# First layer: shift and scale by halves of the features, x's tiles loaded between them, the first half applied meanwhile

## The chip, the cores and the metric

The kernel runs on one core of a Trainium2 chip. The metric is the device time of one execution in microseconds, lower is better. TensorE (PE), VectorE (DVE), ScalarE (ACT), GpSimd (POOL) and the DMA queue of SyncE (SP) each run a program of their own in order and wait for each other by semaphores.

## The reference, cut to what matters

Two layers (`DEPTH = 2`) over 256 context tokens and 1024 latent tokens of 1024 features, batch 1, all in float32. At the head of each layer stands a normalisation with a shift and a scale that are themselves products of a vector with a large weight (`w_mod[l]` is 1024 x 3072, 12.6 MB):

```python
mod = jax.nn.silu(c) @ w_mod[l] + b_mod[l]
mod_c = jax.nn.silu(c_ctx) @ w_mod[l] + b_mod[l]
sh, sc, gt = jnp.split(mod, 3, axis=-1)
sh_c, sc_c, gt_c = jnp.split(mod_c, 3, axis=-1)
hx = _rms(x, norm_w[l]) * (1.0 + sc[:, None, :]) + sh[:, None, :]
hc = _rms(ctx, norm_w[l]) * (1.0 + sc_c) + sh_c
ux = _split(hx @ w_in[l], [M_COLS, A_COLS, G_COLS, D_COLS])
uc = _split(hc @ w_in[l], [M_COLS, A_COLS, G_COLS, D_COLS])
...
x = x + gt[:, None, :] * (yx @ w_out[l])
```

Between the two products four mixers (mLSTM, differential attention, GLA, gated DeltaNet) work on the columns. The change touches only `sh`, `sc`, `hx` and `hc` of the first layer.

## The kernel before, in words

**Order of the program.** The kernel is written as strands (`Strand`, threads at build time). A planner (`Issue`) asks every strand for its next instruction, estimates when its inputs and its engine are ready, and lets the earliest go first, with a rank per strand to break ties (`RANK`). `q_.need(...)` makes a strand wait until another has called `q_.set(...)` of the same name; this orders the program only, the chip waits by the tiles that an instruction reads and writes. All instructions pass through one helper line (L406), so the profile is read by tile names. All loads and stores go through one queue (`dma`, SP), in program order, and a load whose buffer is still in use holds up what stands behind it there. On the chip each load also waits until the load eight places ahead of it has landed, since eight semaphores go round.

**Start of the first layer (`first_norm`).** The 1280 tokens are ten tiles of 128 (tiles 0 and 1 are context), in three groups `GRP` of 2, 4 and 4 tiles. Three strands work side by side:

- `modulations`: `modulation(l, part, c0, n, ...)` makes one part (0 is the shift, 1 the scale, 2 the gate) for `n` features from `c0`. It loads eight row blocks `wm` of `w_mod`, multiplies each with the 2 columns of `cvec` (both vectors, latent and context) into a bank `mod`, copies the two rows to SBUF (`wm`, DVE), turns them with small transposes (PE), and writes columns of `AB[0]` (`md`, then `AB`, DVE). For the first layer the parts 0 and 1 are made whole, 1024 features at a time, with five buffers `wm` of 512 KB.
- `norms`: `normed(t)` loads the tile `x` (three buffers), squares and sums it on ACT (`junk`, `ss`), takes the power -1/2 on POOL (`ss`) and scales `x` on DVE. From the fourth tile on the strand waits for "w_mod loads", that is until the last `wm` load is in the program.
- `turns`: `turn(t, x)` transposes the tile in two times four blocks (`tr<-k_ident,x`, PE) and copies them to `flat[g]` (`f<-tr`, DVE or ACT).

Then the body goes over group and block of 128 features (`todo`, 24 steps): apply scale and shift on DVE (`f<-f,AB`), round on ACT (`hT<-f`, the high part), subtract on POOL or DVE (`hT<-f,hT`, the low part). The order is all eight blocks of a group, then the next group, and the whole loop waits for `(0, "AB")`, both parts.

**What follows (`Proj`).** The projection `mm<-hT,w` multiplies a group's `hT` with the split weights `w`; for one unit of columns that is 24 products per group, group 0 first. A finished bank is copied out by ACT (`st<-mm`) and some of it is stored (`dkr<-st`). After `first_norm` is done, the remaining modulations (gate of the first layer, all of the second) run in 256 KB loads between the products.

Of the kernel before, what the change touches and what calls it, by code (L numbers as in the profile page):

```python
# [22 lines left out]
DM = 1024  # L23
# [12 lines left out]
GRP = ((0, 2), (2, 4), (6, 4))  # L36
# [393 lines left out]
def _build(tc, nc, A, out, root, dbg):  # L430
    q_ = Issue()
# [34 lines left out]
    def mark(label):  # L466
        if q_.me:
            q_.me.label = label

    def dma(dst, src):  # L470
        SP.dma_start(out=dst, in_=src)

    def evac(dst, src, scale=None):
        n = math.prod(src.shape[1:])
        if q_.now["S"] + 0.1 + n / 1200 <= q_.now["V"] + n / 960:
            if scale is None:
                S.copy(dst, src)
            else:
                S.activation(dst, src, AF.Copy, scale=scale)
        elif scale is None:  # L480
            V.tensor_copy(dst, src)
        else:
            V.tensor_scalar(dst, src, scale, None, ALU.mult)

    def sub(dst, a, b):
        n = math.prod(a.shape[1:])
        if q_.now["G"] + 2.2e-3 * n <= q_.now["V"] + n / 960:
            G.tensor_tensor(dst, a, b, ALU.subtract)
        else:
            V.tensor_tensor(dst, a, b, ALU.subtract)  # L490
# [30 lines left out]
    def rsqrt_small(dst, src, mul, eps):  # L521
        V.tensor_scalar(dst, src, mul, eps, ALU.mult, ALU.add)
        shp = list(dst.shape)
        mh = mhalf[:shp[0], 0:1]
        while len(mh.shape) < len(shp):
            mh = mh.unsqueeze(1)
        G.tensor_tensor(dst, dst, mh.to_broadcast(shp), ALU.pow)
# [49 lines left out]
    def pc(l, key, i=0, n=1):  # L577
        return pcol[:, l, PR[key] + i:PR[key] + i + n]
# [27 lines left out]
    AB = [cst([128, 2, 2, 8], f"AB{l}") for l in L2]  # L606

    def xin(l, t):
        if l:
            return x1[t]  # L610
        if t < NCT:
            return A["ctx"][0, 128 * t:128 * t + 128, :]
        return A["x"][0, 128 * (t - NCT):128 * (t - NCT) + 128, :]


    def modulation(l, part, c0, n, p, pps, bufs):

        ps = pps([128, 256], "mod")
        for k in range(8):
            w = p([128, n], "wm", bufs)  # L620
            dma(w, A["w_mod"][l, 128 * k:128 * k + 128, 1024 * part + c0:1024 * part + c0 + n])
            if (l, part, k) == (0, 1, 7):
                q_.set("w_mod loads")
            for j in range(n // 256):
                P.matmul(ps[32 * j:32 * j + 2], cvec[:, k, :], w[:, 256 * j:256 * j + 256],
                         start=(k == 0), stop=(k == 7), tile_position=(0, 32 * j))
        q_.need(("params", l))
        rows = p([128, n], "wm", bufs)[:2].rearrange("p (a b) -> p a b", b=256)
        for j in range(n // 256):
            V.tensor_copy(rows[:, j, :], ps[32 * j:32 * j + 2])  # L630
        if part < 2:
            m, k0 = n // 128, c0 // 128
            pt = pps([128, 256], "mod")
            for j in range(m):
                P.transpose(pt[:, 2 * j:2 * j + 2], rows[:, j // 2, 128 * (j % 2):128 * (j % 2) + 128], ident[:2, :2])
            md = p([128, 8, 2], "md")[:, :m]
            V.tensor_tensor(md, pt[:, :2 * m].rearrange("p (k v) -> p k v", v=2),
                            pc(l, "bm", 8 * part + k0, m).unsqueeze(2).to_broadcast([128, m, 2]), ALU.add)
            for v in range(2):
                if part == 1:  # L640
                    V.scalar_tensor_tensor(AB[l][:, 0, v, k0:k0 + m], md[:, :, v], 1.0, pc(l, "nw", k0, m), ALU.add, ALU.mult)
                else:
                    V.tensor_copy(AB[l][:, 1, v, k0:k0 + m], md[:, :, v])
        else:
            brow = p([128, n], "wm", bufs)[:2]
            dma(brow, A["b_mod"][l:l + 1, 2048 + c0:2048 + c0 + n].to_broadcast([2, n]))
            rv = rows.rearrange("p a b -> p (a b)")
            V.tensor_tensor(rv, rv, brow, ALU.add)
            dma(gtd[l][:, c0:c0 + n], rv)

    def first_norm(hT):

        mark("0norm")
        st3 = ExitStack()
        fp = Pool(st3, "flat", side="right")
        flat = [fp([128, 8, 128 * n], f"f{g}") for g, (t0, n) in enumerate(GRP)]

        def modulations():
            mark("0mod")
            with ExitStack() as st:  # L660
                mp, mps = Pool(st, "wm", side="right"), Pool(st, "mps", PSUM, "right")
                for part in range(2):
                    modulation(0, part, 0, DM, mp, mps, 5)
            q_.set((0, "AB"))
            q_.need((0, "normed"))

            q_.me.rank = RANK["mod"]
            with ExitStack() as st:
                mp, mps = Pool(st, "wm"), Pool(st, "mps", PSUM)
                q_.set((0, "room"))  # L670
                for l, part in ((0, 2), *((l, part) for l in layers if l for part in range(3))):
                    for c0 in (0, 512):
                        modulation(l, part, c0, 512, mp, mps, 3)
                if "d" in parts:
                    q_.need((0, "front"))
            q_.set("modulated")
        q_.spawn(0, modulations)
        if True:
            st2 = ExitStack()
            xp, pps = Pool(st2, "xn"), Pool(st2, "nps", PSUM)  # L680

            def normed(t):
                x = xp([128, DM], "x", 3)
                dma(x, xin(0, t))
                junk = xp([128, DM], "junk")
                ss = xp([128, 2], "ss", 4)
                S.activation(junk, x, AF.Square, accum_out=ss[:, 0:1])
                rsqrt_small(ss[:, 1:2], ss[:, 0:1], 1.0 / DM, EPS)
                V.tensor_scalar(x, x, ss[:, 1:2], None, ALU.mult)
                return x  # L690

            def turn(t, x):
                g = next(g for g, (t0, n) in enumerate(GRP) if t0 <= t < t0 + n)
                o = 128 * (t - GRP[g][0])
                for h in range(2):
                    ps = pps([128, 512], "tr", 2)
                    for i in range(4):
                        P.transpose(ps[:, 128 * i:128 * i + 128], x[:, 128 * (4 * h + i):128 * (4 * h + i) + 128], ident)
                    evac(flat[g][:, 4 * h:4 * h + 4, o:o + 128], ps.rearrange("p (a b) -> p a b", b=128))
            xs = {}  # L700

            def norms():
                mark("0norm")
                for t in range(NT):
                    if t > 2:
                        q_.need((0, "turned", t - 3), "w_mod loads")
                    xs[t] = normed(t)
                    q_.set((0, "normed", t))
            q_.spawn(1, norms)

            def turns():
                mark("0norm")
                for t in range(NT):
                    q_.need((0, "normed", t))
                    turn(t, xs[t])
                    q_.set((0, "turned", t))
            q_.spawn(1, turns)
        q_.need((0, "AB"))
        todo = [(g, k) for g in range(len(GRP)) for k in range(8)]
        for i in range(len(todo) + 2):  # L720
            if i < len(todo):
                g, k = todo[i]
                q_.need((0, "turned", GRP[g][0] + GRP[g][1] - 1))
                x, v = flat[g][:, k, :], 1 if g == 0 else 0
                V.tensor_scalar(x, x, AB[0][:, 0, v, k:k + 1], AB[0][:, 1, v, k:k + 1], ALU.mult, ALU.add)
            if 0 < i <= len(todo):
                g, k = todo[i - 1]
                S.copy(hT[0][g][:, k, :], flat[g][:, k, :])
            if i > 1:
                g, k = todo[i - 2]  # L730
                sub(hT[1][g][:, k, :], flat[g][:, k, :], hT[0][g][:, k, :])
                if k == 7:
                    q_.set((0, "h", g))
        st2.close()
        st3.close()
        q_.set((0, "normed"))
# [463 lines left out]
    def right():  # L1200

        for L in LY:
# [5 lines left out]
            if l == 0:  # L1208
                first_norm(L.hT)
                q_.need("consts")  # L1210
                pst.close()
# [1724 lines left out]
```

## Time and profile before

| | |
|---|---|
| median of 3 runs | 2420.31 us (2413.67 to 2424.84) |
| profiled execution | 2405.2 us, span of the core 2403.3 us |
| mean granted TensorE clock | 0.942 |
| PE busy | 2113.9 us, 88% of the span |
| DVE, ACT, POOL busy | 62%, 41%, 35% |
| DMA | 335.38 MB, mean 140 GB/s |

A group of the profile reads: line, engine, operation, out<-in, count, then busy time, mean time of one, and the idle time of the engine just ahead of it with what ended it. In a timeline row the first number is the start in us and the second the time; a bracket tells how long the engine had been idle and what released it. A matmul of float32 is recorded as two passes.

### The profile page before, as it was taken

The numbers are of one execution on the slowest core, as the hardware profiler recorded it, in microseconds if no ns is written. First come the engines' busy times: TensorE is split into PE (matmuls) and PEld (weight loads), VectorE is DVE, ScalarE is ACT, GpSimd is POOL, SyncE is SP. The second block draws the span as 40 slices with busy tenths as digits, with TensorE's granted clock in tenths as the row PEclk, the third lists the DMA queues.
The fourth block names the chain that finished last, engine by engine and source line by source line (L and its number), as shares of the span: only waits on it lengthen the run. The fifth ranks groups of instructions, "written<-read, shape, count | busy, mean of one in ns | idle before, by whom it ended". The sixth has DMA issues, their size and how long they took to land. (4 is left out here: it accounts for less than half of the span.)

```text
span 2403.3 us, 57716 instructions
## 1 busy us (share of the span) xinstructions
PE 2113.9 (88%) x23367; PEld 1737.7 (72%) x23367; DVE 1500.8 (62%) x2726; ACT 981.6 (41%) x2168; POOL 834.4 (35%) x1048
## 2 busy tenths in 40 slices
PE   5898999999898998888877888889999889976888
PEld 1656778888776677876765668888788667775776
DVE  3586669555386863537666476696633778655475
ACT  2346412433276763213334264313322667632240
POOL 1244523555122224332431244433433122255240
PEclk7899999999999999989989899999999999986999
DMA  7347643445513116258963236433444431164595
GB/s 264 108 140 233 192 147 102 146 146 161 161 44 93 53 51 166 67 128 252 280 214 114 70 108 189 135 113 100 144 124 125 120 98 35 50 170 99 155 302 184
DMA packets 348053, 335.38 MB, mean 140 GB/s; under 512 B 93147, under 2 KB 292283, under 8 KB 347275
## 3 DMA queue, kind: packets, MB, share of 16 engines
q1 hardware_dynamic: 347786, 331.69, 46.1%
q8 instruction: 185, 3.03, 0.5%
q14 instruction: 82, 0.66, 0.1%
HBM read 226.78 MB, written 107.43 MB: 139 GB/s over the span
## 5 line engine op out<-in xcount | busy, mean ns | idle before, releaser
L406 PE MATMUL mm<-w,hT 128*128 128x256 f32 x4512 | 641.2, 293 | 17.6 <-DVE st L406 10.2
L406 PEld LDWEIGHTS mm<-w,hT 128*128 128x128 f32 x4512 | 576.1, 193 | 50.4 <-issue 20.5
L406 PE MATMUL mm<-hT,w 128*128 128x512 f32 (+1 forms) x1680 | 388.8, 377 | 20.3 <-ACT w L406 5.9
L406 PEld LDWEIGHTS mm<-hT,w 128*128 128x128 f32 x1680 | 283.2, 194 | 91.9 <-issue 20.8
L406 DVE TENSOR_REDUCE st<-sc 128x1 f32<-128x1024 f32 (+1 forms) x200 | 200.0, 1026 | 66.8 <-PE sc L406 65.6
L406 ACT ACTIVATE p<-sc,st 128x256 f32<-128x256 f32 (+1 forms) x272 | 211.3, 786 | 68.3 <-DVE st L406 51.7
L406 POOL TENSOR_TENSOR w<-wr,w 128x512 fp32r<-128x512 f32 x54 | 80.7, 1495 | 275.3 <-ACT w L406 220.9
L406 POOL TENSOR_TENSOR hss<-hss,mhalf 128x2 f32<-128x2 f32 (+2 forms) x72 | 104.1, 1446 | 157.1 <-DVE hss L406 143.1
L406 PE MATMUL o<-wo,yT 128*128 128x512 f32 x540 | 148.9, 412 | 4.8 <-DVE x L406 3.2
L406 PE MATMUL sc<-KT,qt 96*128 96x512 f32 (+1 forms) x400 | 124.2, 400 | 29.8 <-DMA KT<-akh 12.9
L406 ACT COPY wt<-tr 128x512 f32<-128x512 f32 (+1 forms) x200 | 102.2, 511 | 66.0 <-PE tr L406 65.6
L406 ACT COPY st<-mm 128x512 f32<-128x512 f32 (+1 forms) x81 | 44.9, 554 | 204.2 <-PE mm L406 142.0
L406 POOL TENSOR_TENSOR ss<-ss,mhalf 128x1 f32<-128x1 f32 (+1 forms) x39 | 68.4, 1754 | 168.9 <-DVE ss L406 168.7
L406 PEld LDWEIGHTS o<-wo,yT 128*128 128x128 f32 x540 | 102.1, 195 | 29.6 <-DVE x L406 3.8
L406 PE MATMUL tr<-k_ident,p 128*128 128x128 f32 x656 | 115.2, 281 | 7.5 <-ACT wt L406 7.0
L406 POOL TENSOR_TENSOR st<-st 128x1 f32<-128x1 f32 (+1 forms) x136 | 27.1, 199 | 270.8 <-ACT p L406 190.4
L406 ACT CAST w<-wr 128x512 fp32r<-128x512 f32 x128 | 77.4, 622 | 98.0 <-PE mm L406 56.7
L406 PE MATMUL po<-wt,av 128*64 128x128 f32 x1312 | 105.3, 284 | 3.5 <-DVE aacc L406 3.5
L406 PEld LDWEIGHTS sc<-KT,qt 96*128 96x128 f32 x400 | 63.6, 196 | 58.9 <-ACT p L406 30.9
L406 DVE SCALAR_TENSOR_TENSOR p<-p,st,p 128x1280 f32<-128x1280 f32 (+1 forms) x72 | 103.0, 1430 | 2.5 <-POOL st L406 2.3
L406 PE MATMUL o<-w,yT 128*128 128x512 f32 x324 | 100.9, 439 | 4.0 <-DVE st L406 4.0
L406 DVE TENSOR_TENSOR w<-wr,w 128x512 fp32r<-128x512 f32 x74 | 68.1, 922 | 54.5 <-ACT w L406 54.3
(314 smaller groups left out, 4062.8 us busy)
## 6 DMA issues: line engine op xcount, KB each, us to landing
wr<-in_w_in SPq DMA_DIRECT2D x64, 512.0 KB
wm<-in_w_mod SPq DMA_DIRECT2D x64, 256.0 KB
y<-y SPq DMA_DIRECT2D x36, 256.0 KB
xp<-st SPq DMA_DIRECT2D x18, 512.0 KB
pd<-rs_NG SPq DMA_DIRECT2D x18, 512.0 KB
kq<-kq SPq DMA_DIRECT2D x18, 512.0 KB
x<-xp SPq DMA_DIRECT2D x18, 512.0 KB
wm<-in_w_mod SPq DMA_DIRECT2D x16, 512.0 KB
```

Of the source, the lines that this page charges most:

```text
L406: r = fn(*a, **k)
```

## The change

The parts 0 and 1 of the first layer are made in two halves of 512 features, shift and scale of the first half, then of the second, with ten buffers of 256 KB in place of five of 512 KB (the same space). The body no longer waits for both parts as a whole: it goes over the halves outermost, and a step needs only its own half (`(0, "AB", k // 4)`) and its group's tiles. The tiles of x no longer wait for the last `wm` load.

```diff
@@ modulation
             dma(w, A["w_mod"][l, 128 * k:128 * k + 128, 1024 * part + c0:1024 * part + c0 + n])
-            if (l, part, k) == (0, 1, 7):
-                q_.set("w_mod loads")
             for j in range(n // 256):
@@ modulations
-                for part in range(2):
-                    modulation(0, part, 0, DM, mp, mps, 5)
-            q_.set((0, "AB"))
+
+                for hf in range(2):
+                    for part in range(2):
+                        modulation(0, part, 512 * hf, 512, mp, mps, 10)
+                    q_.set((0, "AB", hf))
@@ norms
-                        q_.need((0, "turned", t - 3), "w_mod loads")
+                        q_.need((0, "turned", t - 3))
@@ body
-        q_.need((0, "AB"))
-        todo = [(g, k) for g in range(len(GRP)) for k in range(8)]
+        todo = [(g, k) for hf in range(2) for g in range(len(GRP)) for k in range(4 * hf, 4 * hf + 4)]
         for i in range(len(todo) + 2):
             if i < len(todo):
                 g, k = todo[i]
-                q_.need((0, "turned", GRP[g][0] + GRP[g][1] - 1))
+                q_.need((0, "AB", k // 4), (0, "turned", GRP[g][0] + GRP[g][1] - 1))
```

On the queue SP, at the end of the first layer's `wm` loads, the order before is (x_492 is tile 3, x_696 tile 9; dkr is the store of the first finished bank):

```order
L406 DMA wm_484<-in_w_mod 128x1024
L406 DMA wm_490<-in_w_mod 128x1024
L406 DMA x_492<-in_x 128x1024
L406 DMA x_514<-in_x 128x1024
L406 DMA x_542<-in_x 128x1024
L406 DMA x_580<-in_x 128x1024
L406 DMA x_594<-in_x 128x1024
L406 DMA dkr_49_126<-st_661 128x256
L406 DMA x_677<-in_x 128x1024
L406 DMA x_696<-in_x 128x1024
```

Of the change, around the last tiles of x (x_439 is tile 5, x_541 tile 9):

```order
L406 DMA x_439<-in_x 128x1024
L406 DMA x_466<-in_x 128x1024
L406 DMA wm_481<-in_w_mod 128x512
L406 DMA x_490<-in_x 128x1024
L406 DMA wm_495<-in_w_mod 128x512
L406 DMA x_513<-in_x 128x1024
L406 DMA wm_519<-in_w_mod 128x512
L406 DMA x_541<-in_x 128x1024
L406 DMA wm_549<-in_w_mod 128x512
L406 DMA wm_569<-in_w_mod 128x512
```

All ten tiles now stand ahead of the first store, and 21 halves `wm` stand behind the last tile, wm_549 to wm_717; the fifth of them, wm_593, is the last of the first half's scale. The store comes after all of them.

On DVE, from the first half's scale on, the change has (mod_610 is the second half's shift, f_150, f_151 and f_152 are the three groups):

```order
L406 COPY wm_598<-mod_480 2x256 x2
L406 TENSOR_TENSOR md_606<-mod_601,pcol_92 128x8
L406 SCALAR_TENSOR_TENSOR AB_137_214<-md_606,pcol_92 128x4 x2
L406 TENSOR_SCALAR f_150_239<-f_150_239,AB_137_214 128x256 x4
L406 TENSOR_TENSOR hT_142_223<-f_150_239,hT_142_223 128x256
L406 TENSOR_SCALAR f_151_240<-f_151_240,AB_137_214 128x512 x3
L406 TENSOR_TENSOR hT_143_224<-f_151_240,hT_143_224 128x512
L406 TENSOR_SCALAR f_151_240<-f_151_240,AB_137_214 128x512
L406 TENSOR_SCALAR f_152_241<-f_152_241,AB_137_214 128x512
L406 COPY wm_658<-mod_610 2x256
L406 TENSOR_TENSOR hT_143_224<-f_151_240,hT_143_224 128x512
```

and where the first half's applications end:

```order
L406 TENSOR_SCALAR f_152_241<-f_152_241,AB_137_214 128x512
L406 TENSOR_TENSOR md_684<-mod_676,pcol_92 128x8
L406 COPY AB_137_214<-md_684 128x4 x2
L406 COPY wm_721<-mod_688 2x256 x2
L406 TENSOR_TENSOR md_729<-mod_724,pcol_92 128x8
L406 SCALAR_TENSOR_TENSOR AB_137_214<-md_729,pcol_92 128x4 x2
L406 TENSOR_SCALAR f_150_239<-f_150_239,AB_137_214 128x256 x4
L406 TENSOR_TENSOR hT_142_223<-f_150_239,hT_142_223 128x256
L406 TENSOR_SCALAR f_151_240<-f_151_240,AB_137_214 128x512 x3
```

So the twelve applications of the first half stand ahead of the copy of the second half's scale (wm_721). Before, all 24 stood behind both parts, with the scaling of seven tiles of x among them.

On PE the products of group 0 (mm_285) and group 1 (mm_660) before are parted by the transposes of the last three tiles of x:

```order
L406 MATMUL mm_285<-hT_142_223,w_180_329 128x256
L406 MATMUL tr_678<-k_ident_62,x_594 128x128 x4
L406 MATMUL tr_690<-k_ident_62,x_594 128x128 x4
L406 MATMUL tr_702<-k_ident_62,x_677 128x128 x4
L406 MATMUL tr_711<-k_ident_62,x_677 128x128 x4
L406 MATMUL tr_717<-k_ident_62,x_696 128x128 x4
L406 MATMUL tr_723<-k_ident_62,x_696 128x128 x4
L406 MATMUL mm_660<-hT_143_224,w_166_286 128x512 x2
```

With the change all transposes are done before, and the first product (mm_290, group 0) stands behind the second half's scale:

```order
L406 MATMUL tr_573<-k_ident_62,x_541 128x128 x4
L406 MATMUL mod_480<-wm_579,cvec_75 2x256
L406 MATMUL tr_587<-k_ident_62,x_541 128x128 x4
L406 MATMUL mod_480<-wm_579,cvec_75 2x256
L406 MATMUL mod_480<-wm_593,cvec_75 2x256 x2
...
L406 MATMUL mod_688<-wm_717,cvec_75 2x256 x2
L406 MATMUL mod_724<-k_ident_62,wm_721 128x2 x4
L406 MATMUL mm_290<-hT_142_223,w_170_291 128x256 x2
L406 MATMUL mm_290<-hT_142_223,w_171_292 128x256
```

The 24 products of each group then follow without anything between them until late in group 2. Behind the start the planner's decisions shift too: the orders of all engines differ in many places up to the end of the program, with the same 16177 matmuls.

## Rows read from the trace of the kernel before

**Rows 1.** The page: busy time, share of the span and instructions of each engine.

```profile
PE 2113.9 (88%) x23367; PEld 1737.7 (72%) x23367; DVE 1500.8 (62%) x2726; ACT 981.6 (41%) x2168; POOL 834.4 (35%) x1048
```

**Rows 2.** Windows of 50 us: length, PE, PEld, DVE, ACT, POOL busy, granted clock, DMA share, GB/s.

```profile
50.00:100.00 50.00, 37.48 (x185) 29.01 (x186) 35.74 (x64) 25.77 (x50) 19.78 (x22) 0.75 0.32 95
100.00:150.00 50.00, 48.02 (x229) 32.10 (x228) 26.98 (x27) 16.38 (x22) 12.75 (x14) 1.00 0.39 124
200.00:250.00 50.00, 44.84 (x263) 31.72 (x263) 34.64 (x28) 28.08 (x32) 20.59 (x17) 0.97 0.62 201
```

**Rows 3.** The timeline of PE.

```profile
48.59 1.03 PE L406 MATMUL mod<-wm,cvec 128*2 128x256 f32 x8 [0.25 <-DMA wm<-in_w_mod]
...
63.88 1.79 PE L406 MATMUL mm<-hT,w 128*128 128x256 f32 x9
...
79.82 10.58 PE L406 MATMUL mm<-hT,w 128*128 128x512 f32 x40
```

**Rows 4.** The timeline of DVE.

```profile
49.69 1.71 DVE L406 COPY wm<-mod 2x256 f32<-2x256 f32 x4 [11.22 <-PE mod L406]
...
53.11 0.24 DVE L406 SCALAR_TENSOR_TENSOR AB<-md,pcol 128x8 f32<-128x8 f32 x2
...
65.37 1.53 DVE L406 TENSOR_SCALAR f<-f,AB 128x512 f32<-128x512 f32 x1
...
67.42 0.53 DVE L406 TENSOR_SCALAR f<-f,AB 128x512 f32<-128x512 f32 x1
...
89.96 0.68 DVE L406 TENSOR_TENSOR hT<-f,hT 128x512 fp32r<-128x512 f32 x1
```

**Rows 5.** Groups of DVE between 52 and 91 us, shapes apart.

```profile
L406 DVE TENSOR_SCALAR f<-f,AB 128x512 f32<-128x512 f32 x16 | 12.7, 830 | 0.0
L406 DVE TENSOR_SCALAR x<-x,ss 128x1024 f32<-128x1024 f32 x7 | 7.2, 1023 | 2.1 <-POOL ss L406 2.1
L406 DVE TENSOR_TENSOR hT<-f,hT 128x512 fp32r<-128x512 f32 x8 | 6.5, 815 | 0.3 <-ACT hT L406 0.3
L406 DVE COPY f<-tr 128x512 f32<-128x512 f32 x6 | 4.1, 685 | 2.2 <-PE tr L406 2.1
L406 DVE TENSOR_SCALAR f<-f,AB 128x256 f32<-128x256 f32 x8 | 3.8, 506 | 0.0
L406 DVE TENSOR_TENSOR hT<-f,hT 128x256 fp32r<-128x256 f32 x3 | 1.2, 410 | 0.0
```

**Rows 6.** The timeline of SP's queue.

```profile
24.36 19.28 SPq L406 DMA_DIRECT2D wm<-in_w_mod  x13
43.69 16.80 SPq L406 DMA_DIRECT2D x<-in_x  x5
67.99 0.33 SPq L406 DMA_DIRECT2D dkr<-st  x1
68.45 0.83 SPq L406 DMA_DIRECT2D x<-in_x  x2
```

**Rows 7.** The timeline of ACT.

```profile
26.96 1.06 ACT L406 ACTIVATE junk<-x 128x1024 f32<-128x1024 f32 x1 [1.07 <-DMA x<-in_x]
...
72.29 1.06 ACT L406 ACTIVATE junk<-x 128x1024 f32<-128x1024 f32 x1 [1.04 <-DMA x<-in_x]
...
94.92 0.58 ACT L406 COPY st<-mm 128x512 f32<-128x512 f32 x1 [4.23 <-PE mm L406]
```

**Rows 8.** The timeline of PE, the end of one tile's transposes.

```profile
31.00 1.12 PE L406 MATMUL tr<-k_ident,x 128*128 128x128 f32 x4
```

**Rows 9.** The window of the last `wm` loads of 512 KB.

```profile
38.00:48.00 10.00, 6.72 (x56) 0.89 (x56) 0.42 (x3) 0.00 (x0) 0.00 (x0) 0.50 0.99 383
```

**Rows 10.** DMA from 87.7 to 91.5 us in 40 slices, four loads of 256 KB.

```profile
GB/s 0 0 0 0 151 323 366 410 345 453 366 280 173 65 237 108 108 194 280 259 237 345 345 367 367 388 410 323 323 388 367 388 323 367 388 388 410 345 237 194
```

**Rows 11.** Groups of PE between 60 and 95 us, shapes apart.

```profile
L406 PE MATMUL mm<-hT,w 128*128 128x512 f32 x48 | 13.2, 428 | 0.0
L406 PE MATMUL mod<-wm,cvec 128*2 128x256 f32 x12 | 1.8, 378 | 0.4 <-DMA wm<-in_w_mod 0.4
```

## The prediction

> **What bounds the kernel now.** First the page: PE is busy 88% of the span and no other engine over 72% [rows 1]. The windows then tell where PE is not the limit: from 50 to 100 us it works 37.5 of 50 us, from 100 to 150 us 48.0, from 200 to 250 us 44.8 [rows 2]. The change acts in the first 95 us, so the question is when PE gets into its steady run of projections, and whether a lead there lasts.
>
> The timelines of PE, DVE and SP give the chain of the start. Up to 49.6 us the loads of `wm` set the pace: the last modulation product waits for its load and runs from 48.59 [rows 3], and the last ten us move 383 GB/s with the DMA engines 99% busy [rows 9]. The rows are copied at 49.69, and the scale is complete at 53.11 + 0.24 = 53.35 [rows 4]. From there to the last subtraction, which ends at 89.96 + 0.68 = 90.6, is 37.3 us, and DVE is the engine that fills it: applying 12.7 + 3.8, subtracting 6.5 + 1.2, and the late tiles of x 7.2 for scaling and 4.1 for copies out of PSUM [rows 5], together 35.5 us.
>
> PE meanwhile starts group 0 at 63.88, and group 1 only at 79.82 [rows 3]. Group 1's features are not what it waits for; the three last tiles' transposes stand ahead of it in PE's order, and two of those tiles are late. The load of tile 8 was held up in SP's queue behind the store `dkr` of the first bank, which left at 67.99; it went at 68.45 [rows 6] and landed at 72.29 [rows 7]. Group 2's first bank is copied out at 94.92 [rows 7]: that is the moment to beat. Between 79.82 and 94.92 PE also did some 1.8 us of later modulation products [rows 11], so 94.92 - 1.8 = 93.1 compares with a run of products alone.
>
> **The change part by part.** No work is removed: the same 24 applications, the same ten tiles, the same 8.4 MB of `wm`. Added are sixteen more `wm` loads of half the size, small copies and transposes per half, and a later start of `wm` loads behind tiles of x. I follow the new order through the start.
>
> *Loads until the tiles.* Up to the load of tile 3 the queue now carries four halves of `wm` in place of three wholes, so half a MB less; before, the fourth whole left at 24.36 [rows 6]. I let tile 3 leave at 24.4.
>
> *The tiles.* A tile's load takes 72.29 - 68.45 = 3.8 us to land [rows 6, 7]. From landing to the end of its transposes took 31.00 + 1.12 - 26.96 = 5.2 us for tile 2 [rows 7, 8]; then its buffer is free. With three buffers, tile t + 3 leaves 3.8 + 5.2 = 9.0 us after tile t: tile 6 at 33.4, tile 9 at 42.4, ready at 51.4. While SP waits for a buffer the `wm` loads behind it wait too; that is the price of putting x between them.
>
> *The loads behind tile 9.* It and 21 halves are 0.52 + 21 x 0.262 = 6.0 MB. At 383 GB/s [rows 9] that is 15.7 us, so the last one is there at 42.4 + 15.7 + 1 = 59 us, ten later than before. That alone would be a loss; it is paid for by the seven tiles which then are done.
>
> At this point a rule speaks against the change. Four 256 KB loads in flight together ran at 323 to 410 GB/s in the last 17 of the slices before the drop [rows 10], nearly the 383 of the large ones. The Trainium skill, "DMA: Bandwidth & Descriptors", section "Bandwidth", says to batch transfers to at least 1 MiB to get 75% of the peak, and has 341 GB/s for 1 MB and 138 GB/s for 64 KB; 240 GB/s for 256 KB, an estimate of mine halfway between its two figures, would make the 15.7 us into 25 us and bring the last load to 68. The row contradicts it where several loads are in flight, as here; slow loads are one of the rivals, worked out there from rows.
>
> *The first half.* The last of its products stand behind tile 9's transposes on PE, which end at 51.4. Copying the rows took 1.71 for four blocks [rows 4], so 0.9 for two; with the small transposes, half of the 3.66 us from 49.69 to 53.35, I take 2.0 us from product to scale: 53.9 with 0.5 for the products. Hence it is complete no earlier than both halves together were before.
>
> *Applying on DVE.* The 24 applications and 11 subtractions on DVE are 24.2 us [rows 5], so 12.1 for a half. They are stretched: one application of 128x512 takes 0.53 when alone and 1.53 at 65.37 [rows 4], with POOL subtracting at the same time; the mean of 0.83 [rows 5] holds both. With 0.9 for the copy of the shift's rows that stands among them, the first half ends at 53.9 + 13.0 = 66.9. By then the second half's loads are long there (59). The scale's copy stands behind these applications on DVE, so the second scale is complete at 66.9 + 2 = 68.9. This is the new bound: not the loads, but the applications in front of the copy.
>
> *The second half and PE.* Group 0 takes (3.8 + 1.2) / 2 = 2.5 us on DVE, done at 71.4; group 1 (12.7 + 6.5) / 4 = 4.8, done at 76.2; group 2 done at 81.0. PE can begin group 0 at 68, since its first four blocks are ready; it ends at about 72.5, a us behind the last subtraction. A group of 512 columns takes 13.2 / 2 = 6.6 us [rows 11]: group 1 ends at 79.1 and group 2 at 85.7.
>
> *Sum.* 93.1 - 85.7 = 7.4 us earlier. It errs to the safe side, as the cycle of 9.0 us holds a landing in a busy queue and a cold PE, and tile 3 may leave earlier; with 3 us less on the way to tile 9 the sum is 10.4. I take 9. From 100 us on PE is busy 48 of 50 us [rows 2], so the lead is PE's lead and goes on with it; the 5 idle us between 200 and 250 I take to move along. The planner's later decisions differ in many places; I can put no sign on that, only a size, some 6 us either way, the half of the spread of the runs (2413.67 to 2424.84). Profiled execution: 2405.2 - 9 = 2396. It lies 15 us under the median of the runs shown, so the median should go to 2420.3 - 9 = 2411 us, -0.4%.
>
> A change of 0.5%, 12.1 us, is about what can be told from none, so the likeliest is "no difference".
>
> **The rivals.**
>
> *The tiles pass freely and DVE is not stretched: faster, 15 us.* If the tiles keep pace (ready at 47 in place of 51.4, as loads in a less busy queue would give) and an application takes its 0.53 and 0.40 rather than 0.83 and 0.5, a half costs 8.9 us in place of 12.1: first scale at 49.5, second at 61.3, group 0 done at 65, group 2 at 65 + 13.2 = 78.2. That is 93.1 - 78.2 = 15 us, a median of 2405. For it: POOL has nothing else than the subtractions then, and the 7.2 + 4.1 us of x are gone from DVE. Against it: the stretched applications before overlapped just those subtractions, and they stay.
>
> *The loads set the end: faster by 0 to 5 us.* If halves ran all the time at the mean of their row, 1.05 MB in 3.8 us or 276 GB/s [rows 10], the 15.7 us would be 21.8; if a tile's cycle is also 11 us in place of 9, tile 9 leaves at 46.4, the last load is there at 69, the second scale at 72, and group 2 ends 3 us later than forecast: 4 to 5 us of gain, none if the cycle is 13. Median 2415 to 2420. For it: SP waits in order, so a tile's wait is a wait of all loads behind. Against it: the slices of 323 to 410, and the 2 us of slack before DVE would notice even the slow rate alone.
>
> *The tiles go one by one: slower, 15 us.* If the next tile leaves only when the one before it is turned, because loads, squares, scaling and transposes get in each other's way on PE among the modulation products, tiles 5 to 9 take 5 x 9.0 = 45 us from 28: tile 9 at 73 instead of 42.4. The last load then comes at 90, the second scale at 92 and group 2 ends at 108, 15 us later than before: 2435. It decides from the point where tile 9 leaves after about 59: then the second scale comes after 77.6 and group 2 ends after 93.1 + its loss. Against it: one of the three buffers can be filled while two are worked on.
>
> *The lead is lost later: 0.* A later stage waits for something that does not come earlier, or the new order costs what the start gave. Before, PE has few such stages until 250 us [rows 2], but some late in the run. Median 2420, give or take 6.
>
> **How the numbers follow.** The forecast 0.45, the free passage 0.30, loads at the end 0.12, tiles one by one 0.05, lead lost later 0.08. Faster by over 0.5%: nearly all of the free passage (0.27), some of the forecast with a lucky order (0.10) and little of the rest (0.01), 0.38. Slower: the tiles (0.05), and a bad order in the other cases (0.05), 0.10. Same: 0.52. The range reaches from the free passage with an order in its favour (2405 - 8 = 2397) to a lost lead with a little against it (2422).
>
> **What would show it.** Right: the `wm` loads end near 59 us, the second scale on DVE near 69 behind twelve applications, the first `mm<-hT,w` of 128x256 at 66 to 69, group 1 straight behind it, group 2's first `st` copy near 86, all transposes of x done by 52, no `dkr` ahead of an x. Wrong would be: the last `wm` load after 68 with DVE idle before the scale (loads), gaps of 9 us between the tiles' transposes (one by one), applications of 0.53 throughout (free passage), or a lead at 95 us that is gone at 300 or at the end (lost later).

## The result

| | before | after |
|---|---|---|
| median of 16 runs each | 2415.88 us (2409.66 to 2424.84) | 2431.61 us (2424.36 to 2442.05) |
| profiled execution, span | 2403.3 us | 2422.9 us |
| PE busy, rest of the span | 2113.9, 289.4 us | 2116.9, 306.0 us |
| mean granted clock | 0.942 | 0.949 |

The ratio of after to before is 1.0064, with a 95% interval of 1.0052 to 1.0076: the change makes the kernel slower by some 15.5 us. The forecast was 2411 us and "no difference", with 2422 as the upper end of the range. Two slow runs of the experiments below, of 3221 and 6431 us, stand in no ratio.

The page of after answers to [rows 1]: PE does the same work in about the same busy time, 3.0 us more, and stands idle 16.6 us more. Two later executions of before, shown with the experiments, stood idle 295.9 and 300.1 us, so this one pair does not settle how much of the loss is idle time.

```profile
PE 2116.9 (87%) x23367; PEld 1735.0 (72%) x23367; DVE 1500.8 (62%) x2723; ACT 992.9 (41%) x2174; POOL 835.1 (34%) x1059
```

Windows of after, which answer to [rows 2] (length, PE, PEld, DVE, ACT, POOL busy, granted clock, DMA share, GB/s):

```profile
100.00:150.00 50.00, 48.98 (x247) 33.07 (x245) 29.68 (x27) 18.19 (x23) 13.00 (x14) 1.00 0.45 139
150.00:200.00 50.00, 50.00 (x249) 31.74 (x247) 35.90 (x35) 31.30 (x35) 22.22 (x17) 1.00 0.64 205
200.00:250.00 50.00, 36.39 (x205) 25.73 (x203) 29.91 (x24) 31.00 (x34) 19.14 (x14) 0.93 0.56 172
```

From 200 to 250 us PE works 36.4 us, where before had 44.8. The sums from the start, first of before, then of after, tell what that did:

```profile
0.00:200.00 200.00, 158.40 (x808) 99.47 (x808) 114.61 (x151) 82.20 (x123) 58.37 (x68) 0.88 0.55 180
0.00:250.00 250.00, 203.25 (x1071) 131.19 (x1071) 149.25 (x178) 110.28 (x154) 78.96 (x84) 0.90 0.56 184
```

```profile
0.00:200.00 200.00, 164.34 (x850) 101.25 (x850) 114.43 (x159) 85.50 (x124) 65.58 (x71) 0.98 0.58 185
0.00:250.00 250.00, 200.73 (x1052) 126.99 (x1052) 144.34 (x182) 116.50 (x157) 84.72 (x84) 0.97 0.57 183
```

At 200 us the new kernel is ahead, with 42 recorded matmuls more than before; at 250 us it is behind, with 19 fewer.

The start came nearly as forecast. The queue of SP in after, to be held against [rows 6]:

```profile
42.01 0.33 SPq L406 DMA_DIRECT2D x<-in_x  x1
42.39 15.21 SPq L406 DMA_DIRECT2D wm<-in_w_mod  x21
...
77.53 7.96 SPq L406 DMA_DIRECT2D dkr<-st  x2
```

Tile 9 leaves at 42.0 and all ten tiles are ahead of the first store. The 21 halves are issued by 57.6; the DMA engines moved their data until about 62.8. DVE in after, answering to [rows 4]:

```profile
53.77 0.24 DVE L406 SCALAR_TENSOR_TENSOR AB<-md,pcol 128x4 f32<-128x4 f32 x2
...
63.42 0.42 DVE L406 COPY wm<-mod 2x256 f32<-2x256 f32 x1
...
70.69 0.84 DVE L406 COPY wm<-mod 2x256 f32<-2x256 f32 x2 [4.66 <-PE mod L406]
...
72.24 0.24 DVE L406 SCALAR_TENSOR_TENSOR AB<-md,pcol 128x4 f32<-128x4 f32 x2
...
83.93 0.68 DVE L406 TENSOR_TENSOR hT<-f,hT 128x512 fp32r<-128x512 f32 x1
```

The first half's scale is complete at 54.0, the second's at 72.5. Between them DVE stands idle for 4.66 us, waiting for PE. PE in after, answering to [rows 3], shows what PE had waited for itself:

```profile
53.78 3.62 PE L406 MATMUL mod<-wm,cvec 128*2 128x256 f32 x32 [0.26 <-DVE md L406]
63.89 0.58 PE L406 MATMUL mod<-k_ident,wm 2*128 2x2 f32 x4 [6.48 <-DVE wm L406]
65.07 5.57 PE L406 MATMUL mod<-wm,cvec 128*2 128x256 f32 x32 [0.59 <-DVE md L406]
...
71.93 1.87 PE L406 MATMUL mm<-hT,w 128*128 128x256 f32 x13
```

The second row is the second half's shift: its small transposes wait 6.48 us for the copy at 63.42, which stands among the first half's applications on DVE. The 32 products of the second half's scale stand behind these transposes on PE, so they start at 65.07, though their data was there by 62.8. They also take longer than the 32 products of the shift, 5.57 us in place of 3.62. Windows of after (columns as above):

```profile
53.70:57.50 3.80, 3.62 (x32) 1.38 (x32) 3.73 (x9) 1.46 (x4) 2.34 (x3) 1.00 0.84 258
57.50:63.80 6.30, 0.00 (x0) 0.00 (x0) 6.29 (x13) 3.93 (x7) 3.95 (x2) 0.88 0.64 219
63.80:69.00 5.20, 4.52 (x24) 1.79 (x26) 2.17 (x5) 0.62 (x1) 4.59 (x4) 0.50 0.01 3
```

PE did nothing from 57.5 to 63.8, and from there to 69 it was granted a clock of 0.50, the lower of its two levels (1.2 GHz), where it had 1.00 before. The late copy thus cost PE the wait and 1.95 us of slower products.

ACT copies group 2's first bank out here, where [rows 7] have 94.92:

```profile
89.83 0.59 ACT L406 COPY st<-mm 128x512 f32<-128x512 f32 x1 [4.68 <-issue]
```

That is 5.1 us earlier than before. Taking off the 1.8 us of later products that before had done by then [rows 11], and adding the 0.60 us of such products that after did, the lead is 3.9 us, in place of the 7.4 of the sum and the 9 that I took.

As the sums show, a lead is still there at 200 us and gone at 250. In this stretch of after, PE's timeline has

```profile
219.89 1.13 PE L406 MATMUL sq<-raw,bones 128*128 128x512 f32 x2 [2.17 <-POOL raw L406]
...
232.62 1.02 PE L406 MATMUL mod<-wm,cvec 128*2 128x256 f32 x4 [6.00 <-DMA wm<-in_w_mod]
...
240.57 0.60 PE L406 MATMUL mod<-wm,cvec 128*2 128x256 f32 x4 [1.90 <-DMA wm<-in_w_mod]
```

and SP's queue of after shows why the load `wm` came late:

```profile
215.62 6.44 SPq L406 DMA_DIRECT2D wr<-in_w_in  x2
222.16 0.84 SPq L406 DMA_DIRECT2D rs_WI<-rtmp  x2
223.08 0.82 SPq L406 DMA_DIRECT2D K<-dkn  x2
223.96 0.42 SPq L406 DMA_DIRECT2D wm<-in_w_mod  x1
224.42 13.21 SPq L406 DMA_DIRECT2D stage<-rs_X_NCG  x14
237.73 0.37 SPq L406 DMA_DIRECT2D wm<-in_w_mod  x1
```

What holds SP at the second `wr` is a row of SP's waits in after, from 195 to 250 us (us in total, times, longest):

```profile
SPq L406 <- POOL w L406: 5.5, 1, 5.5
```

SP waits 5.5 us until POOL has read the buffer of the second `wr`. The load `wm` of the first product stands behind it, and behind two loads `K` of 640 KB, and leaves at 223.96; that of the second stands behind fourteen `stage` loads, which take SP 13.21 us. Nothing in this stretch was edited. The planner put it in another order, because it decides every instruction by estimated times that had moved in the start. Whether that is the loss, and all of it, is a question for experiments.

### The profile page after: what moved, and what is told of

It is laid out like the page before. It is cut to its first block, busy times and chain, and to the rows that moved or that the text cites. A ratio compares the mean times of both kernels' runs of the same rounds, so it can differ in the third digit from the quotient of the medians.

```text
span 2422.9 us, 57754 instructions
## 1 busy us (share of the span) xinstructions
PE 2116.9 (87%) x23367; PEld 1735.0 (72%) x23367; DVE 1500.8 (62%) x2723; ACT 992.9 (41%) x2174; POOL 835.1 (34%) x1059
## 5 line engine op out<-in xcount | busy, mean ns | idle before, releaser
L406 PE MATMUL mm<-hT,w 128*128 128x512 f32 (+1 forms) x1680 | 394.4, 380 | 20.2 <-ACT hT L406 6.4
L406 ACT COPY wt<-tr 128x512 f32<-128x512 f32 (+1 forms) x200 | 102.4, 512 | 63.0 <-PE tr L406 62.5
L406 PEld LDWEIGHTS tr<-k_ident,p 128*128 128x128 f32 x656 | 76.9, 143 | 37.6 <-ACT wt L406 21.6
```

The costliest lines, as they stand in the source:

```text
L406: r = fn(*a, **k)
```

## The experiments

**How an order is kept.** For the experiments I had the planner write down which strand it chose at each step, and on which engine it put each copy and subtraction that may go to either. A kernel can then be built with a given start and a given order behind it:

```diff
@@ Issue.choose
+        if self.plan is not None:
+            ...
+            s = min(live, key=lambda c: self.plan.get(self.key(c[2]), 1 << 30))[2]
```

"Old order" is that of the kernel before, "new order" that of the changed kernel, from the point on where `first_norm` is done. Except where an expectation says so, nothing is left out.

**Order and start apart.** Theory A: the order that the planner decided anew costs time, and the start gains some. Theory B: the start itself costs the time later on, whatever the order. A2 goes on from A: the order of before is an uncommonly good one, and any that is decided anew is worse. Four kernels, before in the same series at 2415.28 us (17 runs). A ratio, here and below, is estimated from all runs of both kernels, with its 95% interval; it need not be the quotient of the two medians.

New start, old order:

> The start of the change, and behind it every instruction in the order of the kernel before (a recorded list of the planner's choices is followed from the end of first_norm on). Theory A, the order: the start is worth its lead and only the re-decided rest costs, so this is 4 to 6 us faster than before (ratio 0.998), with PE's lead of 4 to 6 us kept to the end of the profile. Theory B, the start: loads or buffers that the new start leaves late cost later whatever the order, so this is 10 to 18 us slower than before, as the change was (ratio 1.004 to 1.0075).

Measured: 2418.43 us, ratio 1.0006 (0.9991 to 1.0021). With the old order the loss is gone, so B falls. There is no gain either, where A expected 0.998. Its PE timeline shows one reason:

```profile
90.88 0.60 PE L594 MATMUL mod<-wm,cvec 128*2 128x256 f32 x4 [2.94 <-DMA wm<-in_w_mod]
```

The old order has later modulation products inside group 2, and their loads stand on SP behind the store of the first bank; PE waits 2.94 us for them. Its start is also 1.6 us later than that of after (the second half's first products start at 55.41 instead of 53.78), so this kernel has no lead at 100 us.

Old start, new order:

> The start of the kernel before, and behind it every instruction in the order of the changed kernel. Theory A, the order: 18 to 22 us slower than before (ratio 1.007 to 1.009), since it has the costly rest without the lead. Theory B, the start: no slower than before by more than 3 us.

Measured: 2439.72 us, ratio 1.0091 (1.0067 to 1.0115), 22 us slower than before without any of the edited lines. The new order costs more than the whole loss; with the new start, ratio 1.0064, it is 6.5 us less, though the two intervals overlap.

Old start, the rest decided anew with all estimated durations two thousandths off. The order was written down from a build with this line, and the kernel run follows it behind the old start:

```diff
@@ Issue.__call__
+        dur *= 1.002      # and 0.998 in the other kernel
```

> The start of the kernel before; the rest is what the planner decides when it takes all its estimated durations 0.2% longer. No work is changed. Theory A1, any order is as good as another give or take: within 6 us of before, either way. Theory A2, the order of the kernel before is an uncommonly good one and another costs: 8 to 25 us slower. Theory B says nothing of it but expects no difference over 5 us.

> As the run with durations 0.2% longer, with 0.2% shorter. Theory A1: within 6 us of before, and not the same side as the other by need. Theory A2: 8 to 25 us slower. Theory B: no difference over 5 us.

Measured: 2438.85 us, ratio 1.009 (1.0062 to 1.0118), and 2452.71 us, 1.0138 (1.0109 to 1.0166). A change of the planner's numbers by 0.2%, which means nothing, costs 22 and 33 us by these ratios; the second is more than the 8 to 25 that A2 expected. A1, a cost within 6 us, falls. With the changed kernel's own, three orders decided anew out of three are worse than that of before, which bears out A2: the order of before is a good one, and the changed kernel lost it. How rare such an order is, so few can't tell.

**Where in the run.** After up to 350 us and the old order behind it, and the reverse:

> The changed kernel exactly as it is up to some 350 us of its span (2303 of 23377 instructions), from there the order of the kernel before for all that is left. Nothing is left out. If the changed order loses its time in one place before 350 us (the wait of 6.0 us for wm at 226 us and its neighbours; TensorE went from 6 us ahead to 5 us behind between 217 and 330 us): median 2425 to 2431, as the changed kernel. If the loss is spread over the order of the whole run: about 2422 to 2425. If it all lies after 350 us: 2410 to 2418.

> The changed kernel's start, then the order of the kernel before up to some 350 us, from there the order of the changed kernel. Nothing is left out. The counterpart of y_new350_old: if the loss lies before 350 us, median 2415 to 2420; if it is spread over the run, 2424 to 2430; if it lies after 350 us, 2428 to 2436.

Measured: 2427.78 us, ratio 1.0043 (1.0025 to 1.006), and 2424.81 us, ratio 1.0034 (1.0019 to 1.0048), before at 2418.35 (31 runs). Against the 1.0006 of the new start with the old order, the first 350 us of the new order cost 0.37%, 9 us, and the rest 0.28%, 7 us. Together 16 us, where the whole costs 1.0064 - 1.0006 = 0.58%, 14 us. By its median the first run lies where its expectation put a loss in one place before 350 us; the second run excludes that, since its interval lies above 1 with the old order up to 350 us. So the loss lies on both sides of 350 us, a good part of it in the first seventh of the run. Which side has more is not told, as each of the two costs is uncertain by some 5 us.

**The waits for `wm` at 226 us.** In both orders each later load is issued one product earlier, from the same three buffers:

```diff
@@ modulation, later parts
-            w = p([128, n], "wm", bufs)
-            dma(w, A["w_mod"][l, 128 * k:128 * k + 128, 1024 * part + c0:1024 * part + c0 + n])
+            while len(ws) <= min(k + 1, 7):
+                ws.append(p([128, n], "wm", bufs))
+                dma(ws[-1], A["w_mod"][l, 128 * len(ws) - 128:128 * len(ws), 1024 * part + c0:1024 * part + c0 + n])
+            w = ws[k]
```

> The changed kernel with its own order, in which each later load wm (gate and second layer) is issued one product earlier, so that it stands ahead of the store and load traffic that held it up (same three buffers, nothing left out). TensorE waits for wm 14.4 us between 60 and 350 us in the changed kernel. Theory (these waits are what the re-decided order loses before 350 us): they fall below 6 us, and the median comes 8 to 10 us down, to 2421 to 2424. Rival (the loss is not there but in many small waits and in the granted clock): the waits for wm fall and the median stays at 2428 to 2433.

> The kernel before with its own order and the same earlier loads wm as in z_ahead_neworder. TensorE waits for wm 8.7 us between 60 and 350 us in the kernel before. If a wait removed there is a wait gained: 4 to 6 us under before. If it is given back later, as the leads of the start: within 2 us of before.

Measured: 2427.84 us, ratio 1.0045 (1.0029 to 1.0061), and 2420.59 us, ratio 1.0017 (0.9999 to 1.0034), before at 2417.34 (26 runs). What PE waits for `wm` between 60 and 350 us (us in total, times, longest), in after

```profile
PE mod L406 <- DMA wm<-in_w_mod: 14.3, 7, 6.0
```

and with the earlier loads

```profile
PE mod L594 <- DMA wm<-in_w_mod: 4.9, 3, 3.3
PE tr L594 <- DMA wm<-in_w_mod: 4.9, 1, 4.9
```

Half of the 9.4 us taken from the products came back as one wait of transposes behind a load `wm`, so 4.5 us were removed. The ratio fell by 0.0019, 4.6 us, but the two intervals overlap, and the median is above the 2421 to 2424 of the theory. The wait at 226 us was shortened, from 6.00 to 3.32 us, not taken away, so this run does not price it. That such waits are not the whole loss is seen in before, which has them too, here in the profiled execution and in w_before_b (below):

```profile
PE mod L406 <- DMA wm<-in_w_mod: 8.7, 11, 2.0
PE mod L406 <- DMA wm<-in_w_mod: 12.4, 13, 2.7
```

After waits for `wm` only 1.9 to 5.6 us more than these. With the old order nothing was gained by the earlier loads.

**What a lead is worth.** With the old order throughout, I changed the length of the start alone.

```diff
@@ modulation, first layer's parts 0 and 1
-            w = p([128, n], "wm", bufs)
-            dma(w, A["w_mod"][l, 128 * k:128 * k + 128, 1024 * part + c0:1024 * part + c0 + n])
+            if l or part > 1 or k % 2 == 0:       # y_lead_less_loads; k == 0 in z_lead_one_load
+                w = p([128, n], "wm", bufs)
+                dma(w, A["w_mod"][l, 128 * k:128 * k + 128, 1024 * part + c0:1024 * part + c0 + n])
```

```diff
+            dma(w, A["w_mod"][1, 128 * k:128 * k + 128, 1024 * part + c0:1024 * part + c0 + n])   # all sixteen, or three of them
             dma(w, A["w_mod"][l, 128 * k:128 * k + 128, 1024 * part + c0:1024 * part + c0 + n])
```

> The kernel before with every second load wm of the first layer's shift and scale left out (each block is multiplied with two rows of cvec, so shift and scale are not the reference's; 4.2 MB less to load in the first 50 us), the rest in the order of before. A lead bought in this way says what one is worth. Both parts should be complete some 8 to 10 us earlier and group 2's first bank copied out 5 to 9 us earlier. Theory (a lead is TensorE's and lives on with an unchanged order): the median is 5 to 9 us under before, 2406 to 2411. Rival (later waits, for loads whose time does not depend on the start, swallow it): the trace shows the lead at 95 us and not at 300 us, and the median is 2413 to 2418.

> The kernel before with only the first of eight loads wm of the first layer's shift and of its scale (this block stands for all eight, so shift and scale are not the reference's; 7.3 MB less to load), the rest in the order of before. The lead at 100 us should be 6 to 10 us (y_lead_less_loads had 4.1). If a lead passes through: the median is 6 to 10 us under before. If it is swallowed: the trace loses it by 430 us, as in y_lead_less_loads, and the median is within 3 us of before.

> The kernel before with three of the sixteen loads wm of the first layer's shift and scale preceded by a second load into the same buffer (overwritten, the result is the same), the rest in the order of before. In z_lag_double_loads sixteen such loads cost 59.5 us at 100 us, so three should cost 8 to 14. If a lag passes through whatever its size: the median is later by what the trace shows at 100 us, 2425 to 2431. If later waits have slack for some 5 us, as they took most of the lead of z_lead_one_load: 2419 to 2425.

> The kernel before with each load wm of the first layer's shift and scale preceded by a load of as much (second layer's rows into the same buffer, overwritten): 8.4 MB more in the start, the rest in the order of before. The result is the same. At 383 GB/s the start is at least 22 us later, more if a load waits for the one ahead of it in its buffer. Theory (TensorE's lead or lag passes through to the end with an unchanged order): the end is later by the same amount that the trace shows at 100 us, 2438 us or more. Rival (later waits swallow it): the lag shrinks in the trace between 100 and 430 us and the median is under 2430.

The fifth kernel, with the start of the change, takes away the wait of 6.48 us that the prediction had missed. It has two edits: the copy moves to ACT, and `mod` has three banks in place of one, so that the products of one part need not wait until DVE has read the bank of the part before:

```diff
@@ modulation
-        ps = pps([128, 256], "mod")
+        mb = 3 if l == 0 and part < 2 else 1
+        ps = pps([128, 256], "mod", mb)
...
-            V.tensor_copy(rows[:, j, :], ps[32 * j:32 * j + 2])
+            (S.copy if l == 0 and part < 2 else V.tensor_copy)(rows[:, j, :], ps[32 * j:32 * j + 2])
...
-            pt = pps([128, 256], "mod")
+            pt = pps([128, 256], "mod", mb)
```

> The changed kernel's start with the first layer's row copies (wm<-mod) on ScalarE in place of VectorE and three banks for mod in place of one, the rest in the order of the kernel before. Nothing is left out. Theory (the copy among the applications held up the scale's 32 products): TensorE's wait of 6.5 us before the small transposes at 65 us is gone, the second scale is complete near 66 to 68 in place of 74.6, group 2's first bank is copied out some 5 us earlier than in x_newstart_oldrest. If a lead at 95 us lives to the end, the median is 5 to 6 us under x_newstart_oldrest's 2418, about 2412. Rival 1 (the applications on VectorE, not the copy, set the second scale): the scale stays at 72 to 74 and the time at 2418. Rival 2 (a lead at the start is swallowed by later waits whatever its size): the scale comes at 67, and the time stays at 2415 to 2420.

Its PE no longer waits long for that copy, and the second half's scale is complete on DVE at 68.9, 5.7 us earlier than the 74.6 of x_newstart_oldrest. The 32 products behind the short waits take 3.62 us, where those of x_newstart_oldrest, behind a wait of 6.49, take 6.10. Which of the two edits gave how much was not run apart.

```profile
61.22 0.28 PE L594 MATMUL mod<-k_ident,wm 2*128 2x2 f32 x2 [1.57 <-ACT wm L594]
62.12 0.28 PE L594 MATMUL mod<-k_ident,wm 2*128 2x2 f32 x2 [0.63 <-ACT wm L594]
62.34 3.62 PE L594 MATMUL mod<-wm,cvec 128*2 128x256 f32 x32
```

```profile
68.66 0.23 DVE L594 SCALAR_TENSOR_TENSOR AB<-md,pcol 128x4 f32<-128x4 f32 x2
```

To read the leads off the traces, two more executions of the kernel before were profiled:

> The kernel before itself, unchanged, for a second profiled execution. If the profiled execution shown of it (span 2403.3 us) is an ordinary one, the matmuls here end within 2 us of it all along and the span is 2402 to 2407. If it was a lucky one, this one drifts behind it from 400 us on, as all kernels with its order did (4 us at 420, 6 to 9 us between 900 and 1200), and the span is 2408 to 2418.

> A third profiled execution of the kernel before. As w_before_a: with both, the drift of one execution against another is known, and with it how much of the loss of a lead in one pair of traces can be told from chance.

Their pages, w_before_a and then w_before_b:

```profile
span 2421.4 us, 57716 instructions
PE 2125.5 (88%) x23367; PEld 1747.1 (72%) x23367; DVE 1499.9 (62%) x2726; ACT 982.1 (41%) x2168; POOL 832.3 (34%) x1048
```

```profile
span 2419.6 us, 57716 instructions
PE 2119.5 (88%) x23367; PEld 1744.7 (72%) x23367; DVE 1498.6 (62%) x2726; ACT 982.0 (41%) x2168; POOL 832.4 (34%) x1048
```

So the execution on which the prediction rests, with a span of 2403.3 us, was a lucky one by 16 to 18 us; at 2405.2 us it was faster than every run of before in any series here. With an unchanged order the end of each matmul can be compared between two traces. The table has the median difference to w_before_b, in us, over the matmuls that end in ten us from the time at the column's head on, and the ratio of the runs:

```
                         100    350*    1200    2390    ratio (95%)
before, as shown        +0.2    -1.5   -10.9   -16.3    same kernel
w_before_a              +1.6    +1.2    +3.4    +1.8    same kernel
x_newstart_oldrest      +2.0    +1.9    -0.4    -6.6    1.0006 (0.9991 to 1.0021)
y_rowcopy_act           -3.8    -5.0    -2.6    -2.9    0.9992 (0.9974 to 1.0010)
y_lead_less_loads       -4.1    -6.7    -6.9    -6.8    0.9992 (0.9975 to 1.0010)
z_lead_one_load        -10.4   -11.8    -4.8    +0.2    0.9977 (0.9961 to 0.9994)
w_lag_three_loads      +13.4   +12.4   +10.2    +3.7    1.0052 (1.0031 to 1.0073)
z_lag_double_loads     +59.7   +57.2   +55.6   +49.7    1.0267 (1.0240 to 1.0293)
* from 340 to 350 us
```

The first two rows are the measure of chance: executions of one kernel stay within some 3 us of each other up to 350 us, and come apart by up to 18 later. A profiled execution need not be a typical one: that of z_lead_one_load was the slowest of its twelve runs, that of z_lag_double_loads the fastest of its six. The medians tell more. A lag of 59.7 us costs 2.67%, 64.5 us; one of 13.4 costs 0.52%, 12.6 us. A lead of 10.4 gives 0.23%, 5.6 us (1.5 to 9.4); leads of 4 give 0.08%, 1.9 us, which is not told from nothing, nor from 4. So lags pass through in full, and a lead of 10 gives about half, or nearly all of it at the edge of its interval. The expectation that a lead is swallowed at 400 us came from comparing with the lucky execution, and isn't borne out.

**One more order decided anew**, behind the start of y_rowcopy_act:

> The changed kernel with the row copies of the first layer on ScalarE and three banks for mod, as y_rowcopy_act, but with the order that the planner decides for it anew. Its lead at 95 us should be 4 to 6 us, as that of y_rowcopy_act. Theory (a newly decided order costs 20 to 37 us against the order of before, whatever set it off, and the start gives back at most 7): 2428 to 2445. Rival (the order of the changed kernel is a bad draw among many even ones): an order decided anew may as well come out at 2405 to 2425.

Measured: 2464.6 us, ratio 1.0185 (1.0156 to 1.0215), before at 2420.52 (17 runs). The same start with the old order has 0.9992, so this order costs 1.93%, 47 us. Its page:

```profile
PE 2136.7 (87%) x23367; PEld 1749.9 (71%) x23367; DVE 1490.8 (60%) x2702; ACT 991.8 (40%) x2183; POOL 839.3 (34%) x1067
```

With its span of 2464.5 us that leaves 327.8 us in which PE doesn't work, against 295.9 and 300.1 in the two later executions of before; PE itself is busy 11 to 17 us longer. All four orders that were decided anew behind a changed number or start (the changed kernel's own, 0.2% up, 0.2% down, this one) cost 14 to 47 us. No version that does the whole work beats the kernel before by what can be told: y_rowcopy_act, the changed start with the copy moved and the old order, is even with it. Its gain over x_newstart_oldrest, 0.14%, is not told from nothing, and its median, 2417.68 us, lies where its second rival put it.

## Why the prediction was wrong

*The step that failed* is the one sentence on the planner: its later decisions "differ in many places; I can put no sign on that, only a size, some 6 us either way". There was a sign, and the size was 14 to 22 us: 1.0064 against 1.0006 with the new start, 1.0091 against 1 with the old. The size had been taken from the spread of the runs, which is a spread of executions of one order and says nothing on another. That a re-decided order is worse rather than even is shown by four of four, two of which have no edit but a factor of 1.002 or 0.998. Of the 24.5 us between the forecast of 9 us gained and the 15.5 lost, the order is 14; the other 10 are the start, which with the old order was worth nothing (1.0006). The rival "lead lost later" had the mechanism in half a sentence ("the new order costs what the start gave") with a price of 0 and a chance of 0.08.

*The loads* were near, in part by luck. Tile 9 left at 42.0 (forecast 42.4), but tile 3 had left at 22.4 instead of 24.4, and from tile 6 to tile 9 it took 11.4 us in place of 9.0. The last `wm` was issued at 57.6 and had landed by 62.8, some 4 us after the forecast 59, which cost nothing, as DVE was not done before 64.8. Between 44 and 58 us the halves ran at 325 GB/s with the DMA engines 93% busy:

```profile
44.00:58.00 14.00, 10.39 (x78) 4.26 (x76) 9.18 (x20) 4.16 (x9) 3.32 (x5) 1.00 0.93 325
```

The Trainium skill, "DMA: Bandwidth & Descriptors", section "Bandwidth", asks for at least 1 MiB per transfer; by my estimate of 240 GB/s halfway between its figures the last load would have come at 68. With many 256 KB loads in flight the row lies above the 240; the 62.8 lies between my 59 and that 68, since from 42 to 62.5 us the mean was 304 GB/s and not 383.

*The first half* was right: scale at 54.0 (forecast 53.9); its applications ended at 64.8 (66.9). *The second half* was 3.6 us late, 72.5 instead of 68.9, though the applications ended 2.1 us early. I had the scale's copy as what stands behind the applications on DVE; it was the shift's copy too, and PE's 32 products behind that. The order of DVE under "The change" shows the shift's copy (wm_658) among the applications; the sum charged it with 0.9 us of DVE and with nothing on PE. "By then the second half's loads are long there" held by 2 us, but the products that use them had not run. They took 5.57 us, 1.95 of it by the lower clock, of which the sum had nothing either. These 3.6 us are nearly all of the 4.1 by which group 2 ended after its forecast (89.83 against 85.7), and of the missing lead (3.9 in place of 7.4). y_rowcopy_act bears this out, with the copy moved away and three banks: the scale came 5.7 us earlier.

*The 1.6 us on top* of the sum, from 7.4 to 9, had no row of its own, and came to nothing.

*The lead goes on with PE*: borne out for lags, in part for leads, as far as an unchanged order goes.

*The execution profiled* lay 15 us under the median of the runs shown, as the prediction said. Against w_before_b it was lucky mostly after 900 us, and against both later executions by no more than 3 us in the first 350, so this did not hurt the sum.

Open is why the order of before is so much better. Its price lies on both sides of 350 us. It is not all idle time of PE: the kernel with 0.2% longer durations stands idle 297.2 us, as much as before (289.4 to 300.1), and is busy 2138.3 us, 13 to 24 us longer; w_rowcopy_ownorder stands idle 327.8. Of the many waits only those for `wm` were tried, and their price is not settled.

## What to carry to other kernels

Where a planner decides the order from estimates, an edit at the start is two edits: the start, and a new order of everything behind it. Price the second by deciding the order anew from numbers two thousandths off, and measure the first with the old order kept; then keep whichever order is good. When work is cut in halves, follow on each engine what stands behind the second half's first small step, since an in-order engine passes a late copy on to whatever is queued behind its reader.

## What was not expected of the hardware

Three profiled executions of one kernel had spans of 2403.3, 2421.4 and 2419.6 us at granted clocks of 0.942, 0.936 and 0.940. They agree within 3 us up to 350 us, so a loss of a few us later than that can't be placed by one pair of traces. A lag cost its full length, while a lead of 10.4 us gave back 5.6 (1.5 to 9.4). And a wait of 6.5 us cost more than itself: the 32 products behind it ran at a granted clock of 0.50 and took 5.57 us in place of 3.62.
